# Plain sums in DRAM for three operand sets, merge gates loaded ahead, and later pool differences in a fused attention and pooling layer

## The chip, the cores and the metric

The kernel runs on one core of one Trainium2 chip. The metric is device time in microseconds (us) of the whole program. Before the change it took 1887.97 us, the median of 3 runs (1885.35 to 1888.47).

## The reference, cut to what matters

One layer over x (2048 x 1024): a modulated input u, one wide projection of u, sliding-window attention and a multi-scale causal pooling beside each other, each gated and projected, merged by sigmoid gates, projected out and normalized.

```python
u = x * (1.0 + scale[:, None, :]) + shift[:, None, :]
h = u @ w_in[l]
q, k, v, a_gate, p_in, p_gate, m_a, m_p = jnp.split(h, offsets, axis=-1)
a = sliding_window_sink_attention(q, k, v, sinks[l], bias, mask) * jax.nn.silu(a_gate)
a = a @ w_attn_proj[l]
p = jnp.einsum('bsgc,gcd->bsgd', multiscale_causal_pool(p_in), w_pool_mix[l]).reshape(B, S, POOL_WIDTH)
p = (p * pool_scale[l]) * jax.nn.silu(p_gate)
p = p @ w_pool_proj[l]
y = jax.nn.sigmoid(m_a) * a + jax.nn.sigmoid(m_p) * p
y = (y @ w_out[l]) * (1.0 + gate[:, None, :])
x = layer_norm(DEEPNORM_ALPHA * x + y, ln_gain[l], ln_bias[l])
```

The pooling subtracts from a mean over the last 2, 4, 8 or 16 positions (by group of channels) the value itself.

## The kernel before

**Products.** Every large matrix product is done in f32 precision from two fp32r parts, hi and lo, with three matmuls for each pair of 128x128 weights and 128x512 operand (`mm3`). The operand side is laid out as *sets*: seven sums of quarters of a matrix (B11, T1, T2, B21, T3, B22, T4), so that four output pieces come from seven products in place of eight. A set is a tile of 128 x 4 x 2 x 512: four row blocks, hi and lo. One product of a set is 12 matmuls. There is one buffer for each set, so a set of the next stage is filled when the last product of this stage has read it. The weight side is a *quad* (`class Quad`): W and A22 are loaded, POOL makes the sums (`sum1`, `mid`, `late`), and `pair_split` or `half_split` makes hi on ScalarE (ACT) and lo on VectorE (DVE) into tiles named w_set.

**Stages.** head; a first ring (g0) of five groups of two quads over the first half of the sequence; attention (a0); a second ring (g1) for the second half, with the two last gate quads of the first half in front of it ("post"); attention (a1); then "mix": the post quads, attention projection and pool projection of the first half (ain0, pin0) and of the second (ain1, pin1), and the output projection (wo) with the normalization. u1, ain0, pin0, ain1, pin1, wo also name the DRAM stores of the operands of those stages; g1 works on u1.

**The order in a ring.** `back` runs the products of a group: T2 and B21 of both quads, then T3 and B22 of each, then T4, 10 in all; `front` runs B11 and T1 of the next group's two quads. After each product comes a tick, and tables hang work on ticks: `sums_to` (four row blocks for each store, some 13 ticks each) loads two tiles named spare, second_qs or second_kk, lets POOL make the T sums in place and puts the results into a store; `planned` fills the sets of the next stage by `PLAN`. A store is either *split* (u1, wo, ain0: hi and lo in DRAM, made by `kept_parts`, into k_hi and k_lo from the ring "c" of five buffers unless a "parts" room is free; fetched by `fill_set` with 1 MB a transfer) or *plain* (pin0, ain1, pin1: f32 sums, 512 KB a fetch, cast by ACT and subtracted by DVE in the set itself, at the ticks of `FETCH_AT` and `SPLIT_AT`). The gate tiles (sig, ga, gp) use the ring "c" as well. Engines called through `act`, `dve`, `pool`, `sp` keep the program's order; calls through `nc` may be moved by the scheduler. Nearly all transfers are issued by SyncE (SP), one after the other.

**Attention.** 64 units of two heads and 128 queries, with 3 more to drain, interleave scores, softmax, transposes and values with steps of filler quads: pool input ("mix"), gates, and q. A mix quad gives four pieces. `take_p` handles one: `first` copies it from PSUM with 16 columns of history into vb (ACT) and POOL adds shifted copies, one to four times by window, into a tile "fin"; `second`, a unit later, has DVE subtract the piece from the mean and POOL multiply by the gate; a unit later it is stored to pin. `pool_free` starts pieces at least a unit apart. `seed` copies into a fresh PSUM bank, for which the bank of the quad's second piece must be free (`free_b`). There are four PSUM banks "mm". `take_gate` copies a gate's piece into a tile "raw", from where it is stored.

**Merge.** In mix, `attn_quad` and `pool_quad` load, for each of four output pieces, a stored gate (ma or mp), apply a sigmoid where it was stored raw, and multiply the piece by it, all at the piece's own place.

Of the kernel before, what the change touches and what calls it, by code (L numbers as in the profile page):

```python
# [12 lines left out]
F32 = mybir.dt.float32  # L13
# [46 lines left out]
def kernel(  # L60
# [56 lines left out]
    def split_store(name):  # L117
        return {n: dp.tile([4, P, 2, CH], F32, name=f"{name}_{n}_split") for n in set_names}

    u1_d = split_store("u1")  # L120
    wo_d = split_store("wo")
    ain0_d = split_store("ain0")
# [76 lines left out]
    def fill_set(name, half, src, eng=None):  # L199

        dst = as32(sets[name][:, 2 * half : 2 * half + 2])
        (eng or nc.sync).dma_start(dst, src[2 * half : 2 * half + 2].rearrange("i p h c -> p i h c"))

# [3 lines left out]
    def kept_parts(ph, dst, src):  # L207

        t = []

        def split():
            at = ph.turn_of("parts")
            if at:
                t.extend(at)
            else:
                t.extend(ph.c(n, F32R) for n in ("k_hi", "k_lo"))
            act.copy(t[0], src())
            low(dve, t[1], src(), t[0])

        def keep():  # L220
            for h in range(2):
                sp.dma_start(dst[:, h, :], as32(t[h]))

        return split, keep

    def sums_to(ph, store, i, load, work=None):

        b, split_too = [], store["B11"].shape[0] == 4
# [22 lines left out]
        raw = () if not split_too else ((4, "B11", (0, 0)), (5.4, "B21", (1, 0)), (6.1, "B22", (1, 1)))  # L251
        for at, name, z in (
            *raw, (8.5, "T1", (0, 1)), (10, "T2", (1, 1)), (11.5, "T4", (1, 0)), (13, "T3", (0, 0)),
        ):
            if split_too:
                split, keep = kept_parts(ph, store[name][i], lambda z=z: x(*z))
                todo += [(at, split), (at + 1, keep)]
            else:
                todo.append((at + 0.6, lambda name=name, z=z: put(sp, store, name, i, x(*z))))
# [10 lines left out]
    class Quad:  # L270
# [4 lines left out]
        def __init__(self, srcs, consume):  # L275
            self.srcs, self.consume = srcs, consume
# [319 lines left out]

    def attn_quad(s, m):
        def consume(ph, mi, t, src):
            k = m + mi
            g = ph.c("ga")  # L600
            nc.sync.dma_start(g, gates_d["ma"][s, k, t])
            nc.scalar.activation(g, g, AF.Sigmoid)
            if k not in ta:
                ta[k] = wide(ph, k)
            nc.vector.tensor_tensor(ta[k][:, t * CH : (t + 1) * CH], src, g, ALU.mult)

        return Quad((wap[m], wap[m + 1]), consume)

    def pool_quad(s, m):
        def consume(ph, mi, t, src):  # L610
            g = ph.c("gp")
            nc.sync.dma_start(g, gates_d["mp"][s, m + mi, t])
            if m < 4:
                nc.scalar.activation(g, g, AF.Sigmoid)
# [7 lines left out]
        return Quad((wpp[m], wpp[m + 1]), consume)  # L622
# [127 lines left out]
    def attention(ph, s, fills, post, opened):  # L750
# [28 lines left out]
        def pool_sums(m, t, acc):  # L779
            g = m // 2  # L780
            w = POOL_W[g]
            vb = tp.tile([P, 16 + CH], F32, tag="vb", bufs=1, name="vb")
# [17 lines left out]
            return cur  # L800

        pool_free, free_b = [0], [0]
# [4 lines left out]
        def take_p(m, t, acc):  # L807
            n = pool_free[0] = max(now_n[0], pool_free[0] + 1)
            x = []

            def first():
                x.append(ld("pg", gates_d["pg"][s, m, t], 2))
                x.append(pool_sums(m, t, acc))
# [745 lines left out]
```

## Time and profile before

| | |
|---|---|
| median of 3 runs | 1887.97 us |
| profiled execution | 1886.14 us |
| its span, first to last instruction | 1884.3 us |
| mean granted TensorE clock | 0.958 |
| PE, DVE, ACT, POOL busy | 91%, 65%, 52%, 56% |
| moved by DMA | 378.75 MB, mean 201 GB/s |

PE is TensorE, PEld its weight loads; POOL is GpSimd; SPq is SyncE's queue of instructions that issue transfers. Line L56 is a helper that records operations, so groups are told by their tiles: `mm<-set_B,w_set` is a product with one of the B sets into a bank of the ring "mm", `lg<-set_T,w_set` one with a T set. A number in brackets behind a row of the timeline is the idle time of the engine before it, with what ended it.

### The profile page before, as it was taken

What the parts mean: (1) busy time and instruction counts of PE and PEld (TensorE: products, weight loads), DVE (VectorE), ACT (ScalarE), POOL (GpSimd) and SP (SyncE); (2) the same over time, 40 slices, a digit from 0 to 9 for tenths busy, and PEclk for the clock granted to TensorE, in tenths of its full rate; (3) what the DMA queues carried; (4) which work ended last, traced back from release to release, by engine and by line L of the source; (5) the groups of instructions that cost most, each with busy time, mean ns of one, the idle gap of its engine ahead of it and who ended that gap; (6) DMA issues with size and microseconds to landing.
All of it is one profiled execution on the core that took longest, in us unless ns stands there. A gap on an engine that the chain in (4) does not pass through costs nothing.

```text
span 1884.3 us, 24950 instructions
## 1 busy us (share of the span) xinstructions
PE 1713.3 (91%) x8056; PEld 1418.5 (75%) x8056; DVE 1231.1 (65%) x2270; ACT 974.2 (52%) x2044; POOL 1062.8 (56%) x810
## 2 busy tenths in 40 slices
PE   6899999999998975749999999998998989999997
PEld 6688778888787864537888887887876767878785
DVE  6977756767675554655657777676346566755777
ACT  4644556767575532334457776665425334622452
POOL 2253438677768443545457859587365665354542
PEclk9999999999998997879999999999999989999998
DMA  8589753233423598788343234323899586779532
GB/s 325 190 280 333 226 187 122 92 107 129 140 80 111 202 326 288 277 283 298 115 164 128 96 111 140 102 90 118 295 381 333 162 288 221 245 241 381 199 134 101
DMA packets 199666, 378.75 MB, mean 201 GB/s; under 512 B 19424, under 2 KB 45168, under 8 KB 199536
## 3 DMA queue, kind: packets, MB, share of 16 engines
q1 hardware_dynamic: 196416, 372.91, 57.4%
q10 hardware_dynamic: 3088, 4.23, 0.9%
q8 instruction: 64, 1.05, 0.2%
q14 instruction: 66, 0.54, 0.1%
q0 software_dynamic: 32, 0.02, 0.0%
HBM read 245.79 MB, written 134.44 MB: 202 GB/s over the span
## 4 chain that ended last, share of the span: by engine, by line
PE 32%; POOL 6%; DMA 6%; DVE 5%; issue 3%; ACT 1%; SPq 1%; POOLq 0%; DVEq 0%; ACTq 0%
PE mm L56 20%; PE lg L56 10%; DVE w_set L135 1%; PE pv L56 1%; PE pt L56 1%; POOL w_set L56 1%; POOL nxt L56 1%; POOL fin L56 1%; DMA ain_T<-spare 1%; DMA W<-in_wpp_dram 1%; POOL wide L617 1%; ACT w_set L325 1%; DMA spare<-ain_B 1%; DMA A<-in_wap_dram 0%; DMA W<-in_wap_dram 0%
## 5 line engine op out<-in xcount | busy, mean ns | idle before, releaser
L56 PE MATMUL mm<-set_B,w_set 128*128 128x512 f32 x2664 | 681.0, 403 | 55.4 <-ACT w_set L325 29.7
L56 PEld LDWEIGHTS mm<-set_B,w_set 128*128 128x128 f32 x2664 | 508.2, 194 | 176.1 <-ACT w_set L325 33.4
L56 PE MATMUL mm<-set_T,w_set 128*128 128x512 f32 x1824 | 464.0, 401 | 27.8 <-DVE mm L56 12.5
L56 PE MATMUL lg<-set_T,w_set 128*128 128x512 f32 x1728 | 433.4, 402 | 46.0 <-DMA set_T<-u_T_split 15.7
L56 PEld LDWEIGHTS lg<-set_T,w_set 128*128 128x128 f32 x1728 | 333.2, 194 | 125.6 <-ACT lg L368 16.2
L56 PEld LDWEIGHTS mm<-set_T,w_set 128*128 128x128 f32 x1824 | 341.0, 191 | 103.9 <-DVE mm L56 16.9
L135 DVE TENSOR_TENSOR w_set<-W,w_set 128x1024 fp32r<-128x1024 f32 x138 | 197.6, 1432 | 202.7 <-ACT w_set L325 184.1
L56 POOL TENSOR_TENSOR w_set<-W,w_set 128x512 fp32r<-128x512 f32 x160 | 208.8, 1312 | 158.2 <-ACT w_set L56 152.7
L325 ACT CAST w_set<-W 128x1024 fp32r<-128x1024 f32 x138 | 144.6, 1049 | 263.8 <-PE mm L56 151.8
L288 POOL TENSOR_TENSOR W<-W,A 128x512 f32<-128x512 f32 x46 | 68.8, 1495 | 314.2 <-ACT sig L585 64.3
L56 ACT ACTIVATE L<-L,nm 128x257 f32<-128x257 f32 (+1 forms) x256 | 127.1, 498 | 27.6 <-DVE nm L56 21.9
L56 POOL TENSOR_TENSOR spare<-spare 128x512 f32<-128x512 f32 x68 | 117.1, 1724 | 28.1 <-DVE spare L56 13.0
L297 POOL TENSOR_TENSOR W<-W 128x512 f32<-128x512 f32 x46 | 66.9, 1455 | 109.8 <-DVE w_set L135 100.6
L56 DVE CUSTOM_DVE_ANT_0 L<-lg,bt,nsink 128x256 f32<-128x256 f32 (+1 forms) x256 | 111.6, 473 | 20.2 <-PE lg L56 10.9
L56 DVE COPY o<-pv 64x256 f32<-64x256 f32 x128 | 54.3, 424 | 105.4 <-PE pv L56 104.0
L56 ACT CAST pth<-pt 128x512 fp32r<-128x512 f32 (+1 forms) x128 | 72.9, 569 | 81.5 <-PE pt L56 81.0
L56 ACT ACTIVATE L<-L,sm 128x256 f32<-128x256 f32 (+1 forms) x128 | 64.3, 503 | 94.6 <-DVE sm L56 94.3
L56 ACT CAST w_set<-W 128x512 fp32r<-128x512 f32 (+1 forms) x164 | 100.4, 626 | 23.6 <-POOL W L56 10.0
L56 POOL TENSOR_TENSOR W<-W 128x512 f32<-128x512 f32 x82 | 105.1, 1296 | 4.2
L292 POOL TENSOR_TENSOR W<-W 128x512 f32<-128x512 f32 x44 | 74.0, 1682 | 43.2 <-DVE w_set L135 33.5
L56 DVE TENSOR_TENSOR ptl<-pt,pth 128x512 fp32r<-128x512 f32 (+1 forms) x128 | 85.7, 669 | 5.6 <-ACT pth L56 5.5
L293 POOL TENSOR_TENSOR W<-W 128x512 f32<-128x512 f32 x44 | 71.8, 1631 | 23.4 <-DMA W<-in_win_dram 18.6
(232 smaller groups left out, 2464.0 us busy)
## 6 DMA issues: line engine op xcount, KB each, us to landing
W<-in_win_dram SPq DMA_DIRECT2D x42, 512.0 KB, 5.6
W<-in_win_dram SPq DMA_DIRECT2D x42, 256.0 KB, 3.8
A<-in_win_dram SPq DMA_DIRECT2D x42, 256.0 KB, 4.1
ag_d<-sig SPq DMA_DIRECT2D x32, 256.0 KB, 4.7
pg_d<-sig SPq DMA_DIRECT2D x32, 256.0 KB, 4.4
pg<-pg_d SPq DMA_DIRECT2D x32, 256.0 KB, 3.1
pin_B<-fin SPq DMA_DIRECT2D x32, 256.0 KB, 2.1
ag<-ag_d SPq DMA_DIRECT2D x32, 256.0 KB, 3.0
```

The costliest lines, as they stand in the source:

```text
L56: return lambda *args, **kw: self.tc.keep_in_program_order(op(*args, **kw))
L135: engine.tensor_tensor(dst, src, as32(hi), ALU.subtract)
L288: e.tensor_tensor(self.w[:, 1, :], self.w[:, 2, :], self.a22, ALU.add)
L292: e.tensor_tensor(x[:, 1, :], x[:, 1, :], x[:, 0, :], ALU.subtract)
L293: e.tensor_tensor(x[:, 2, :], x[:, 0, :], x[:, 2, :], ALU.subtract)
L297: e.tensor_tensor(x[:, 3, :], x[:, 3, :], x[:, 1, :], ALU.subtract)
L325: a.copy(by_two(hi), raw)
L617: nc.gpsimd.tensor_tensor(dst, g, dst, ALU.add)
```

## The change

1. u1, wo and ain0 are kept as plain sums. `kept_parts`, `fill_set` and the "parts" rooms are gone; their sets are fetched and split by the path that pin0, ain1 and pin1 had. `sums_to` stores B11, B21 and B22 too where it worked on them (u1, wo), and stores at slightly other ticks.
2. `back` first calls `ahead` of each quad: the group's eight merge gates are loaded together, and their sigmoids made, into a ring of 8 buffers (5 before).
3. `take_p`: for windows of 8 and 16 the subtraction comes two units after `first`. A piece also starts at least three units after the one before the last. The quad's second piece is subtracted from its copy in vb (now two buffers), and `free_b` is a unit earlier. "raw" has no buffer of its own; it shares the two of "fin".

```diff
-    u1_d = split_store("u1")
-    wo_d = split_store("wo")
-    ain0_d = split_store("ain0")
+    u1_d = set_store("u1")
+    wo_d = set_store("wo")
...
-        raw = () if not split_too else ((4, "B11", (0, 0)), (5.4, "B21", (1, 0)), (6.1, "B22", (1, 1)))
+        made = ((4, "B11", (0, 0)), (5, "B21", (1, 0)), (6, "B22", (1, 1))) if work else ()
         for at, name, z in (
-            *raw, (8.5, "T1", (0, 1)), (10, "T2", (1, 1)), (11.5, "T4", (1, 0)), (13, "T3", (0, 0)),
+            *made, (8.6, "T1", (0, 1)), (10.1, "T2", (1, 1)), (11.6, "T4", (1, 0)), (13.1, "T3", (0, 0)),
         ):
-            if split_too:
-                split, keep = kept_parts(ph, store[name][i], lambda z=z: x(*z))
-                todo += [(at, split), (at + 1, keep)]
-            else:
-                todo.append((at + 0.6, lambda name=name, z=z: put(sp, store, name, i, x(*z))))
+            todo.append((at, lambda name=name, z=z: put(sp, store, name, i, x(*z))))
...
     def back(ph, grp, opened, nxt, own, tick):
         st = []
+        for turn in range(2):
+            for q in grp:
+                if q.ahead:
+                    q.ahead(ph, turn)
...
-        if store["B11"].shape[0] == 4:
-            return [(p, lambda n=n, h=h: fill_set(n, h, store[n])) for p, n, h in PLAN]
...
+    def gates_ahead(name, s, m, raw):
+        g = {}
+
+        def ahead(ph, turn):
+            for mi, t in (((0, 0), (1, 1)), ((0, 1), (1, 0)))[turn]:
+                x = g[mi, t] = ph.c("g")
+                sp.dma_start(x, gates_d[name][s, m + mi, t])
+                if raw:
+                    nc.scalar.activation(x, x, AF.Sigmoid)
+
+        return g, ahead
...
-            vb = tp.tile([P, 16 + CH], F32, tag="vb", bufs=1, name="vb")
+            vb = tp.tile([P, 16 + CH], F32, tag="vb", bufs=2, name="vb")
...
-            n = pool_free[0] = max(now_n[0], pool_free[0] + 1)
+            n = max(now_n[0], pool_free[1] + 1, pool_free[0] + 3)
+            pool_free[:] = pool_free[1], n
+            wait = 1 if POOL_W[m // 2] < 8 else 2
+            own = (m % 2, t) == (0, 1)
...
-                dve.scalar_tensor_tensor(p, p, 1.0 / POOL_W[m // 2], acc, ALU.mult, ALU.subtract)
+                dve.scalar_tensor_tensor(
+                    p, p, 1.0 / POOL_W[m // 2], copied if own else acc, ALU.mult, ALU.subtract
+                )
                 pool.tensor_tensor(p, p, pg, ALU.mult)
-                later(n + 2, lambda: keep_raw(pin_d[s], m, t, p))
-
-            later(n + 1, second)
-            if (m % 2, t) == (0, 1):
-                free_b[0] = n + 1
+                later(n + wait + 1, lambda: keep_raw(pin_d[s], m, t, p))
+
+            later(n + wait, second)
+            if own:
+                free_b[0] = n
...
-                x = tp.tile([P, CH], F32, tag="raw", bufs=1, name="raw")
+                x = tp.tile([P, CH], F32, tag="fin", bufs=2, name="raw")
...
-        ph.turns["parts"] = cycle([[cols(x, n) for n in range(2)] for x in kq[2:]] + [None])
+        ph.turns["spare"] = cycle([None, None, *(as32(x) for x in kq[2:])])
...
-    with Pools("mix", spare=4, p=2, c=5) as ph:
+    with Pools("mix", spare=4, p=2, c=8) as ph:
```

Where instructions stand now. First ACT in g1, at the end of the first group and the opening of the next (sig: a gate's piece; w_set: a hi part of weights, from W or from A; k_hi: a hi part that is stored; second_qs, second_kk: tiles that `sums_to` works on). Before:

```order
L585 ACTIVATE sig<-mm 128x512
L56 CAST k_hi<-second_qs_6624 128x512
L56 CAST k_hi<-second_qs_6626 128x512
L325 CAST w_set<-W 128x1024
L585 ACTIVATE sig<-p_6952 128x512
L56 CAST k_hi<-second_qs_6624 128x512
L585 ACTIVATE sig<-mm 128x512
L56 CAST k_hi<-second_qs_6627 128x512
L56 CAST k_hi<-second_kk 128x512
L369 COPY p_7391<-mm 128x512
L325 CAST w_set<-W 128x1024
```

After:

```order
L56 CAST set_T_573<-set_T_573 128x2x512
L555 ACTIVATE sig<-mm 128x512
L293 CAST w_set<-W 128x1024
L56 CAST set_T_573<-set_T_573 128x2x512
L293 CAST w_set<-W 128x1024
L555 ACTIVATE sig<-mm 128x512
L555 ACTIVATE sig<-p_6821 128x512
L300 CAST w_set<-A_6615 128x512
L555 ACTIVATE sig<-mm 128x512
L300 CAST w_set<-A_6662 128x512
```

The k_hi casts between the weight splits are gone, and the last of the 14 casts of the set splits stand there; the groups behind this one have neither.

Next DVE in the first attention stage, at the end of the mix quad with window 16 (mm<-mm,p is the addition behind the product T2, fin the pool difference, sm, o and L,nm the softmax and output steps of a unit). Before:

```order
L56 TENSOR_TENSOR mm<-mm,p_5971 128x512
L56 SCALAR_TENSOR_TENSOR fin<-fin,p_5623 128x512
L56 RECIPROCAL sm<-sm 128x2
L56 COPY o_6087<-pv 64x256
L56 TENSOR_TENSOR o<-pv,o_6087 64x128 x2
L56 ISA L,nm<-lg,bt,nsink 128x256
```

After:

```order
L56 TENSOR_TENSOR mm<-mm,p_5847 128x512
L56 SCALAR_TENSOR_TENSOR fin<-fin,mm 128x512
L56 RECIPROCAL sm<-sm 128x2
L56 COPY o_5962<-pv 64x256
L56 TENSOR_TENSOR o<-pv,o_5962 64x128 x2
L56 ISA L,nm<-lg,bt,nsink 128x256
```

At this place the fourth piece's difference (from p) stood; now the third's (from mm) stands there, and the fourth's follows two units later.

Last SP in the mix stage, at the first groups of ain0 (ga and g: merge gates; ain_T<-spare: stores of T sums of the second half; W and A: weights of the next group). Before:

```order
L281 DMA W<-in_wap_dram 128x512
L282 DMA A_13343<-in_wap_dram 128x512
L283 DMA W<-in_wap_dram 128x2x512
L601 DMA ga<-ma_d 128x512 x2
L56 DMA ain_T_119<-spare 128x512
L281 DMA W<-in_wap_dram 128x512
L282 DMA A_13389<-in_wap_dram 128x512
L283 DMA W<-in_wap_dram 128x2x512
L601 DMA ga<-ma_d 128x512
L56 DMA ain_T_123<-spare 128x512
L601 DMA ga<-ma_d 128x512 x2
```

After:

```order
L56 DMA ain_T_111<-spare 128x512
L56 DMA ain_T_115<-spare 128x512
L56 DMA g<-ma_d 128x512 x8
L56 DMA ain_T_113<-spare 128x512
L56 DMA spare<-ain_B_112 128x512
L56 DMA spare<-ain_B_114 128x512
L249 DMA W<-in_wap_dram 128x512
```

The gate loads, spread over the group in ones and twos, now stand as one block of eight ahead of the weight loads of the next group.

More of the change, by code (lines that the diff above doesn't have):

```diff
@@ L197, in split_set @@
         low(d, lo, src, hi)
-    def fill_set(name, half, src, eng=None):
-        dst = as32(sets[name][:, 2 * half : 2 * half + 2])
-        (eng or nc.sync).dma_start(dst, src[2 * half : 2 * half + 2].rearrange("i p h c -> p i h c"))
     def put(q, store, name, i, src):
         q.dma_start(store[name][i // 2, :, i % 2, :], src)
[L207 to L214, printed above, removed]
-            else:
[L216 to L224, printed above, removed]
     def sums_to(ph, store, i, load, work=None):
-        b, split_too = [], store["B11"].shape[0] == 4
+        b = []
         def x(r, c):
@@ L1390, in second_phase @@
             ))
-        for raw, split in ((ain_d[0], ain0_d), (pin_d[0], pin_d[0])):
+        for raw in (ain_d[0], pin_d[0]):
             for i in range(4):
-                side.append(sums_to(ph, split, i, load_raw(raw, i)))
+                side.append(sums_to(ph, raw, i, load_raw(raw, i)))
         ahead, hooks = hooks, {}
```

33 lines of the change are left out of this document (13 added, 20 removed).

## The prediction

> **What bounds the kernel now.** I read the page, then one windows table over the stages, then the waits and the timeline where TensorE (PE) stands. A row of the table gives: stretch in us, its length, busy us (instructions) of PE, PEld, DVE, ACT and POOL, granted PE clock, DMA share, GB/s.
>
> ```profile
> span 1884.3 us, 24950 instructions
> ```
> ```profile
> 80.00:280.00 200.00, 191.50 (x930) 159.39 (x928) 146.71 (x168) 104.33 (x163) 84.92 (x51) 1.00 0.81 269
> 280.00:640.00 360.00, 345.59 (x1825) 295.82 (x1826) 245.93 (x700) 235.72 (x655) 272.13 (x226) 0.98 0.34 110
> 640.00:680.00 40.00, 39.98 (x178) 32.83 (x177) 17.84 (x22) 16.91 (x24) 14.52 (x10) 1.00 0.96 338
> 680.00:880.00 200.00, 133.00 (x473) 100.92 (x472) 115.30 (x118) 71.43 (x111) 89.10 (x57) 0.82 0.85 291
> 880.00:960.00 80.00, 79.07 (x343) 64.49 (x344) 45.41 (x52) 35.76 (x55) 37.30 (x29) 0.98 0.52 174
> 960.00:1320.00 360.00, 345.98 (x1847) 295.60 (x1846) 247.76 (x696) 240.70 (x656) 267.21 (x215) 0.99 0.34 112
> 1320.00:1440.00 120.00, 115.82 (x506) 93.89 (x504) 53.67 (x62) 44.86 (x63) 57.67 (x40) 0.99 0.90 331
> 1440.00:1600.00 160.00, 137.17 (x551) 108.73 (x550) 104.01 (x93) 69.51 (x92) 106.79 (x63) 0.91 0.72 246
> ```
>
> PE is the bound nearly everywhere: it is idle 8.5 us of 200 in the first ring stage (g0, 80 to 280), 14.4 and 14.0 us in the two attention stages (280 to 640, 960 to 1320). It is not the bound from 680 to 880, in the second ring stage (g1): 133.0 busy of 200, at a granted clock of 0.82. No other engine is full there either; the DMA engines are at 0.85.
>
> What g1 should take follows from its products of 12 matmuls, here its first two and its last in the timeline of PE (start, us, what):
>
> ```profile
> 644.55 2.88 PE L56 MATMUL lg<-set_T,w_set 128*128 128x512 f32 x12
> 647.27 2.88 PE L56 MATMUL mm<-set_B,w_set 128*128 128x512 f32 x12
> ...
> 962.57 2.88 PE L56 MATMUL mm<-set_T,w_set 128*128 128x512 f32 x12
> ```
>
> Undisturbed, products start 2.72 us apart. By the code g1 has 10 + 4 of the two carried-over quads and the first group's front, 5 x 10 of the groups, and 4 x 4 + 2 of the following fronts: 82, or 223 us. From 644.55 to the end of the last, 965.29, it took 320.7: **97 us lost**. 67 of them are the idle time in 680 to 880, the rest mainly the slow clock behind the gaps. Who is waited for there (engine and line <- releaser, us, times, longest), for PE and for the queue that issues transfers (SPq):
>
> ```profile
> PE mm L56 <- ACT w_set L325: 24.0, 4, 8.5
> PE lg L56 <- DMA set_T<-u_T_split: 15.7, 4, 7.0
> ```
> ```profile
> SPq L56 <- DVE k_lo L56: 55.3, 35, 6.0
> SPq L56 <- ACT k_hi L56: 27.5, 21, 4.8
> ```
>
> The queue stood 82.8 us for hi and lo parts that the kernel stores, with the weight loads behind them in it. One such place, in the timeline (in brackets the idle time before, and what ended it):
>
> ```profile
> 739.99 1.27 POOL L288 TENSOR_TENSOR W<-W,A 128x512 f32<-128x512 f32 x1 [24.75 <-DMA A<-in_win_dram]
> ...
> 749.48 0.62 ACT L56 CAST k_hi<-second_kk 128x512 fp32r<-128x512 f32 x1 [4.46 <-DMA wo_T_split<-k_lo]
> ...
> 758.29 4.19 PE L56 MATMUL mm<-set_B,w_set 128*128 128x512 f32 x8 [7.79 <-ACT w_set L325]
> ```
>
> POOL had to wait for a weight load; ACT, in order, held a k_hi cast until an earlier store had released a ring buffer, with the weight split that PE needs behind it.
>
> **The change part by part.** A. *Plain sums instead of parts.* A tile of 128x512 f32 is 256 KB; a set (8 tiles split, 4 plain) is 2.1 MB split and 1.05 MB plain. In g1, reading seven u1 sets saves 7.3 MB, storing seven wo sets 7.3 MB, and ain0 shrinks from 14.7 MB to 4.2 (the T sets alone; its B sets stand in DRAM already). That is 25.2 MB of the 85.6 that rows 640 to 960 moved (338 x 40 + 291 x 200 + 174 x 80 us). The 60.4 MB left are 246 GB/s over 246 us, below the 269 at which g0 lost 8.5 us in 200. Also gone from g1 are 56 k_hi casts, 56 k_lo subtractions and 68 of 112 store issues; new are 14 set splits, which cost what today's plain sets do (ns: min/median/max):
>
> ```profile
> L56 DVE TENSOR_TENSOR k_lo<-second_qs,k_hi x28: 677/692/1778, 693.9 to 860.5; 128x512 fp32r<-128x512 f32 x28
> ```
> ```profile
> L56 ACT CAST set_T<-set_T x24: 1027/1046/1052, 1423.7 to 1649.2; 128x1024 fp32r<-128x1024 f32 x24
> L56 DVE TENSOR_TENSOR set_T<-set_T x24: 1207/1218/2321, 1426.4 to 1655.8; 128x1024 fp32r<-128x1024 f32 x24
> ```
>
> At medians DVE sheds 56 x 0.69 = 39 us and takes on 14 x 1.22 = 17; since neither DVE nor ACT is near full, only the order matters. What stays of the 97 us: 10, at g0's rate of loss over 246 us; 11 in the opening, whose first 18 products (49 us) ask for u1 7.3 MB, wout 4, wo stores about 4, weights and gates about 5 (counted in the code), 20 MB, and at 338 GB/s that is 60 us; 6 for set splits that stand before other work. 27 stay, **70 gained**. Ends: 38, if each of the opening's seven sets comes as late as the longest wait for one above (49 in place of 11 and 6, rounded), and 87, if the opening is hidden.
>
> Fetches of both sizes have rows (KB each, median us to landing):
>
> ```profile
> set_T<-u_T_split SPq DMA_DIRECT2D x8, 1024.0 KB, 8.7
> ...
> set_T<-pin_T SPq DMA_DIRECT2D x16, 512.0 KB, 5.7
> ```
>
> Half the bytes land in 66% of the time, not 50. Counted by landing, reading u1 saves 34% of 14.7 MB, 5.0 MB in place of 7.3; 2.3 MB at 291 GB/s are 8 us, and A is 62. I keep 70, since SP issues ahead and what a full queue delays is bytes; 62 lies in the range.
> The Trainium skill, DMA: Bandwidth & Descriptors (Bandwidth), advises batches of at least 1 MiB for 75% of peak, which speaks against halving these fetches. The trace agrees in direction.
>
> In g0, 28 tiles fewer are split and half the bytes stored: 2 us of its 8.5, ends 0 and 6.
>
> B. *Pool differences.* In attention DVE waits in order for the running sums on POOL, four adds long where the window is 16 (waits of the whole span, then the timeline):
>
> ```profile
> DVE fin L56 <- POOL fin L56: 55.2, 18, 6.5
> ```
> ```profile
> 582.56 0.69 DVE L56 SCALAR_TENSOR_TENSOR fin<-fin,mm 128x512 f32<-128x512 f32 x1 [4.91 <-POOL fin L56]
> ...
> 587.02 1.65 PE L56 MATMUL mm<-set_T,w_set 128*128 128x512 f32 x3 [4.80 <-DVE mm L56]
> ```
>
> Behind it on DVE are the softmax steps and the addition that PE waits for. A unit later (360 us / 67 units, 5.4 us) the sum is done, as 4.91 is less than a unit. A quad's first piece then keeps its PSUM bank until unit 33 (mix 4, taken in 31), and PE begins the product that reuses it in 34: covered by a unit; without that cover PE would wait what DVE waits now. The second piece's bank is free after ACT's copies. Next late are the sums' buffers: "raw" now shares the two of "fin", so ACT's raw copies (units 6, 7, 36, 39, 56, 59 of each stage) and POOL's fourth sum wait for a store issued in the same or the next unit. No row shows this; it is between 0 and the 4.80 of PE above, at 12 places. I take 0.5 each, since PE's weight splits run three products ahead: 28.4 us of idle time become 7 left over and 6 of these, **15 gained**; ends -30 (12 x 4.80 against the 28.4) and 24.
>
> C. *Gates a group ahead; splits at ain0 and wo* (waits of ACT, then the timeline):
>
> ```profile
> ACT gp L614 <- DMA gp<-mp_d: 30.8, 8, 7.7
> ACT ga L602 <- DMA ga<-ma_d: 22.6, 10, 6.2
> ```
> ```profile
> 1456.55 1.21 DVE L56 TENSOR_TENSOR set_B<-set_B 128x1024 fp32r<-128x1024 f32 x1
> ...
> 1460.69 4.63 PE L56 MATMUL mm<-set_T,w_set 128*128 128x512 f32 x12 [5.38 <-DVE wide L605]
> ```
>
> From 1320 to 1600 PE is idle 27.0 us. ACT's 53 us of waiting for gates go, most of them off PE's path: I take 10 of the 27. The lighter queue in 1320 to 1440 (0.90 busy, 331 GB/s) gives 3 of the 4.2 there. Against it, ain0 and wo bring 14 splits each to stage changes that had none. At 1460 PE waited for a gate product that stood on DVE behind set splits such as the one at 1456; half of that 5.38 at two changes is -5. **8 gained**; ends -10 (both whole, no gain from gates) and 22.
>
> **The sum.** 70 + 2 + 15 + 8 = 95. The profiled execution took 1886.1 us (the span and 1.8 around it): 1791. The median of the runs shown, 1888.0, lies 1.9 above it: **1793**.
>
> **Rivals.** *Everything goes* (0.12): A 87, g0 6, B 20, C 15, so 1760. For it: 60.4 MB at 338 GB/s need 179 of 246 us. Against: the opening asks for more than that rate.
>
> *Set splits hold ACT and DVE* (0.15). They stand in program order, fetched only three or four products ahead, and beside them each side slows: set_T subtractions took 1218 ns at the median and up to 2321. If 28 of the 42 new ones each lose that 1.1 us on PE's path, it is 31, so 1824. For it: the row 1440 to 1600, 22.8 us idle around two such stage changes. Against: in 1320 to 1440 DVE is busy 54 of 120.
> The Trainium skill, SBUF — State Buffer (Who interferes with whom), has a DVE operation with two SBUF inputs and a POOL operation that reads SBUF exclude each other. The trace agrees, with its 2321 against 1218.
>
> *The shared buffers cost what the later difference saves* (0.10): 12 places at 3.8 us are 45 where I count 6; B is -24 and the time 1832. Against: the store is issued within a unit of its sum.
>
> *Slower* (0.04): eight gate loads stand as a block in SP's order at the head of eight groups, ahead of weight loads, and the last needs the buffer that the group before releases with its last consumer. If that blocks, weights come late as at 739.99 and PE waits 7.79 as at 758.29. At 16 quads it decides from 95 / 16 = 5.9 us each; at 7.79 it is 125, so 1918. Against: that consumer is some four products (11 us) before the block.
>
> **How the numbers follow.** The forecast, with its own range of 1765 to 1815, holds 0.59; the rivals have the chances above. I give 1793 and the range 1762 to 1838: it takes in the forecast, the second and third rival and the upper part of the first. 0.2% (4 us) is about what a measurement of this kernel can tell from no change. Faster 0.95, same 0.01, slower 0.04.
>
> **What would show it.** Right: in g1 no gap of PE over 4 us after its first 60; SP's waits for k_lo and k_hi gone; DVE's wait for fin under 15 us; ACT's for gates under 15. Wrong: in g1's opening ACT waiting over 20 us for set fetches, and PE for w_set behind it; ACT raw or POOL fin waiting for a pin_B store; POOL W waiting for weights behind "g" loads. Above 1856 (B and C at their lower ends) A itself has failed.

## The result and the profile after

The changed kernel takes 1762.21 us, the median of 4 runs (1761.71 to 1762.30), against 1886.66 us before (4 runs): a ratio of 0.9345, interval 0.9324 to 0.9365. The profiled execution took 1762.15 us. So 124 us went where the forecast had 95. The time stands 31 us below the number given, 0.2 us above the lower end of the range, and 3 us below the 1765 to 1815 that the forecast took as its own.

To see where it went, both traces are laid beside each other product by product: the products are the same and stand in the same order, so a stage is the time from the start of its first product to the start of the next stage's first. "Attention" is both attention stages.

| us | head | g0 | attention | g1 | mix | span |
|---|---|---|---|---|---|---|
| before | 80.6 | 198.6 | 731.4 | 322.1 | 551.6 | 1884.3 |
| after | 81.3 | 191.4 | 716.2 | 242.9 | 528.5 | 1760.3 |
| gained | -0.7 | 7.1 | 15.2 | 79.2 | 23.1 | 124.0 |
| predicted | 0 | 2 | 15 | 70 | 8 | 95 |

First the stretches of after, in the windows table (columns as in the prediction: stretch, length, busy us and instructions of PE, PEld, DVE, ACT, POOL, granted clock, DMA share, GB/s). Its third to fifth row are g1:

```profile
80.00:271.00 191.00, 189.02 (x926) 159.02 (x925) 120.17 (x137) 88.16 (x131) 79.43 (x50) 1.00 0.73 239
271.00:632.00 361.00, 350.34 (x1856) 298.72 (x1855) 248.80 (x707) 239.95 (x661) 278.02 (x228) 0.98 0.35 114
632.00:672.00 40.00, 40.00 (x177) 32.98 (x177) 28.08 (x26) 26.91 (x35) 15.28 (x10) 1.00 0.94 337
672.00:792.00 120.00, 108.60 (x454) 87.99 (x453) 75.41 (x69) 39.78 (x57) 98.73 (x62) 0.96 0.83 294
792.00:873.00 81.00, 81.00 (x363) 67.06 (x362) 42.67 (x53) 37.20 (x57) 31.69 (x23) 1.00 0.46 151
```

g1 moves 61.0 MB (337 x 40 + 294 x 120 + 151 x 81 us) where the prediction counted 60.4. In g1 PE stands only in the middle row, for 11.4 us, and the clock there is 0.96 where it was 0.82. The first and last product of g1, and the two long gaps, in the timelines of PE and of DVE (in brackets the idle time before, and what ended it):

```profile
631.83 2.88 PE L56 MATMUL lg<-set_T,w_set 128*128 128x512 f32 x12
...
677.59 4.38 PE L56 MATMUL mm<-set_B,w_set 128*128 128x512 f32 x11 [4.49 <-DVE set_B L56]
...
695.09 4.29 PE L56 MATMUL mm<-set_B,w_set 128*128 128x512 f32 x11 [4.71 <-DVE set_B L56]
...
870.61 2.88 PE L56 MATMUL mm<-set_T,w_set 128*128 128x512 f32 x12
```
```profile
670.80 4.53 DVE L56 TENSOR_TENSOR second_qs<-second_qs,cb 128x1024 f32<-128x1024 f32 x2
675.26 2.28 DVE L56 TENSOR_TENSOR set_B<-set_B 128x1024 fp32r<-128x1024 f32 x1
```

From 631.83 to 873.33 (the last start and 2.72) it is 241.5 us for 82 products, 18.5 over the ideal 223, where 97 were lost before. At both gaps PE waits for a set split that stands on DVE behind the scaling of wo. It does not wait for a fetch: ACT waits for those of u1 1.3 us (T sets) and 0.8 us (B sets) in all.

Then the waits of the whole span that the prediction named (engine, line <- releaser: us, times, longest):

```profile
DVE fin L56 <- POOL fin L56: 6.2, 6, 2.0
ACT g L575 <- DMA g<-ma_d: 9.6, 5, 5.3
ACT g L575 <- DMA g<-mp_d: 3.1, 1, 3.1
ACT set_T L56 <- DMA set_T<-u_T: 1.3, 2, 0.9
ACT raw L56 <- DMA pin_B<-fin: 31.9, 5, 9.3
```

DVE's 55.2 us for the running sums are 6.2, ACT's 53 us for gates are 12.7, and the fetches of u1's T sets make ACT wait for 1.3; SP's waits for k_lo and k_hi are gone with these tiles. Of the signs of being right one is missed by little: the second long gap of PE in g1 ends 63.3 us into it. The last row is new, and the prediction had named it as a sign of being wrong: ACT waits for a store of pool differences before it may write raw. One such place in attention, in the timelines of ACT and PE:

```profile
470.59 0.59 ACT L56 COPY raw<-mm 128x512 f32<-128x512 f32 x1 [7.77 <-DMA pin_B<-fin]
...
472.87 0.56 ACT L56 CAST pth<-pt 128x512 fp32r<-128x512 f32 x1
```
```profile
473.49 0.58 PE L56 MATMUL pv<-pth,vv 128*128 128x256 f32 x1 [3.61 <-ACT pth L56]
```

Behind the raw copy on ACT stand a weight split, the copies of the next pool piece and the softmax's pth, and PE waits 3.61 us for that.

### The profile page after: what moved, and what is told of

The parts are those of the page before. It is cut to its first block, busy times and chain, and to the rows that moved or that the text cites. A ratio compares the mean times of both kernels' runs of the same rounds, so it can differ in the third digit from the quotient of the medians.

```text
span 1760.3 us, 24568 instructions
## 1 busy us (share of the span) xinstructions
PE 1673.0 (95%) x8056; PEld 1396.0 (79%) x8056; DVE 1219.1 (69%) x2228; ACT 964.7 (55%) x2002; POOL 1087.6 (62%) x810
## 4 chain that ended last, share of the span: by engine, by line
PE 42%; POOL 8%; DVE 7%; DMA 5%; issue 4%; ACT 3%; SPq 0%; POOLq 0%; DVEq 0%; ACTq 0%
PE mm L56 27%; PE lg L56 12%; PE pv L56 2%; DVE w_set L131 2%; PE pt L56 1%; POOL spare L56 1%; POOL w_set L56 1%; POOL wide L597 1%; DMA set_T<-ain_T 1%; DVE set_T L56 1%; POOL W L256 1%; DMA W<-in_wpp_dram 1%; POOL fin L56 1%; DMA g<-mp_d 1%; DVE set_B L56 1%
## 5 line engine op out<-in xcount | busy, mean ns | idle before, releaser
L56 PE MATMUL mm<-set_B,w_set 128*128 128x512 f32 x2664 | 665.0, 397 | 21.9 <-DVE set_B L56 9.2
L56 PEld LDWEIGHTS mm<-set_B,w_set 128*128 128x128 f32 x2664 | 501.8, 191 | 134.1 <-DVE w_set L131 11.4
L56 PE MATMUL mm<-set_T,w_set 128*128 128x512 f32 x1824 | 457.8, 397 | 7.2 <-POOL w_set L56 4.1
L56 PE MATMUL lg<-set_T,w_set 128*128 128x512 f32 x1728 | 422.6, 395 | 18.3 <-DVE w_set L131 9.2
L56 PEld LDWEIGHTS mm<-set_T,w_set 128*128 128x128 f32 x1824 | 337.3, 189 | 79.4 <-POOL w_set L56 6.3
L56 PEld LDWEIGHTS lg<-set_T,w_set 128*128 128x128 f32 x1728 | 325.6, 190 | 93.5 <-DVE w_set L131 14.5
L56 ACT ACTIVATE L<-L,nm 128x257 f32<-128x257 f32 (+1 forms) x256 | 127.1, 498 | 21.9 <-DVE nm L56 15.6
L265 POOL TENSOR_TENSOR W<-W 128x512 f32<-128x512 f32 x46 | 73.1, 1589 | 99.4 <-DVE w_set L131 88.2
L56 POOL TENSOR_TENSOR spare<-spare 128x512 f32<-128x512 f32 x64 | 112.6, 1762 | 5.1 <-DVE spare L56 2.2
L56 POOL TENSOR_TENSOR W<-W 128x512 f32<-128x512 f32 x82 | 109.8, 1352 | 4.2
L260 POOL TENSOR_TENSOR W<-W 128x512 f32<-128x512 f32 x44 | 73.4, 1672 | 40.7 <-DVE w_set L131 31.6
L261 POOL TENSOR_TENSOR W<-W 128x512 f32<-128x512 f32 x44 | 75.6, 1718 | 22.2 <-DMA W<-in_win_dram 14.3
L56 DVE TENSOR_SCALAR L<-L,sm 128x256 f32<-128x256 f32 (+1 forms) x128 | 88.9, 695 | 0.0
```

What stands on the lines that cost most here:

```text
L56: return lambda *args, **kw: self.tc.keep_in_program_order(op(*args, **kw))
L260: e.tensor_tensor(x[:, 1, :], x[:, 1, :], x[:, 0, :], ALU.subtract)
L261: e.tensor_tensor(x[:, 2, :], x[:, 0, :], x[:, 2, :], ALU.subtract)
L265: e.tensor_tensor(x[:, 3, :], x[:, 3, :], x[:, 1, :], ALU.subtract)
```

## The experiments

All times of a run's stages are in one table, worked out as above; the medians are of 4 runs or 5.

| us | median | g0 | attention | g1 | mix |
|---|---|---|---|---|---|
| sums_alone | 1780.98 | 190.2 | 730.7 | 244.2 | 535.5 |
| pool_alone | 1871.59 | 197.6 | 715.8 | 322.6 | 551.3 |
| gates_alone | 1873.62 | 199.2 | 730.7 | 322.3 | 540.8 |
| no_gates | 1770.26 | 191.7 | 716.4 | 245.3 | 534.4 |
| bytes_back | 1795.31 | 190.8 | 715.3 | 275.2 | 529.2 |
| casts_back | 1787.56 | 190.1 | 715.9 | 268.7 | 528.9 |
| both_back | 1821.02 | 193.4 | 716.6 | 298.2 | 528.9 |
| hi_only | 1816.62 | 197.5 | 732.4 | 268.0 | 534.1 |
| raw_nxt2 | 1749.70 | 190.8 | 702.7 | 242.9 | 528.7 |
| wait_1 | 1763.15 | 190.4 | 715.2 | 243.5 | 527.7 |
| early_first | 1760.76 | 191.0 | 716.6 | 244.5 | 525.6 |
| best | 1761.69 | 192.5 | 701.6 | 243.3 | 541.0 |

**The three parts alone.** sums_alone is the kernel before with part 1 of the change (stores, sums_to, set_steps, the spare rooms, ain0's phase):

```diff
...
-    u1_d = split_store("u1")
-    wo_d = split_store("wo")
-    ain0_d = split_store("ain0")
+    u1_d = set_store("u1")
+    wo_d = set_store("wo")
...
```

> The kernel before with the plain sums alone (u1, wo, ain0 as f32 sums, split where used); the pool differences and the gates as they were. The traces of before and after, laid beside each other product by product, give the gain of the whole change as 7.1 us in g0, 79.0 in g1, 15.2 in the two attention stages and 23.0 in mix. If the parts add up (main theory), this one has g0 and g1 whole, nothing in attention, and in mix at most what its smaller ain0 and wo fetches bring: 1795 to 1805 us, g1 near 242 us. My prediction's size for it, 72 gained, would be 1815. Rival: the plain sums need the later pool differences or the gates ahead to pay, since 42 new set splits stand among the waits that those remove; then g1 stays over 260 us or mix gets slower, and the time is 1815 to 1840.

Measured: 1780.98 us, ratio 0.9433 (0.9398 to 0.9468): 104.5 us below before, more than either theory. g0 and g1 have their whole gain without the other parts, so the rival falls. And mix gains 16.1 of its 23.1, although it has 28 of the new set splits and the gates are as they were.

pool_alone has part 3 alone (take_p, vb, free_b, raw in the buffers of fin):

```diff
...
-            n = pool_free[0] = max(now_n[0], pool_free[0] + 1)
+            n = max(now_n[0], pool_free[1] + 1, pool_free[0] + 3)
...
-                x = tp.tile([P, CH], F32, tag="raw", bufs=1, name="raw")
+                x = tp.tile([P, CH], F32, tag="fin", bufs=2, name="raw")
```

> The kernel before with the later pool differences alone. Main theory: 15 us of the gain, as the two attention stages show in the traces (365.4 to 359.1 and 366.0 to 357.2), so 1871 to 1873 us, g1 unchanged near 320. Rival: part of those 15 us comes from what the plain sums left behind at the border of the stages (fewer transfers still running when attention begins), then 1876 to 1883.

Measured: 1871.59 us, ratio 0.9919 (0.9889 to 0.9950), 13.9 us; attention gains 15.6, g1 and mix stay. The part stands by itself. Its waits already show both sides of it, as in after:

```profile
DVE fin L56 <- POOL fin L56: 6.2, 6, 2.0
ACT raw L56 <- DMA pin_B<-fin: 32.1, 4, 9.2
```

gates_alone has part 2 alone, and no_gates, run later, is the kernel after without it:

```diff
...
+        for turn in range(2):
+            for q in grp:
+                if q.ahead:
+                    q.ahead(ph, turn)
...
-    with Pools("mix", spare=4, p=2, c=5) as ph:
+    with Pools("mix", spare=4, p=2, c=8) as ph:
```

> The kernel before with the merge gates loaded a group ahead alone (ring of 8 buffers in mix). Theory one: the 23 us that mix gained (551.6 to 528.5) are the gates', as PE no longer waits behind gate loads on ACT and DVE: 1862 to 1866 us. Theory two (the prediction's sizes): gates bring about 13 and the rest of mix's gain belongs to the smaller ain0 and wo sets: 1872 to 1876. Rival: the block of eight loads on SP takes back what it saves where the set fetches stand behind it: 1880 or more.

> The kernel after with the merge gates loaded at their own places as before, in a ring of 5. Laid apart, mix takes 551.6 us before, 535.5 with the plain sums alone, 540.8 with the gates alone and 528.5 with both. Theory one, the gates are worth 7 us beside the plain sums: 1767 to 1771 us, mix near 535.5. Theory two, what the gates gained alone (11 to 12) holds here too and the difference in the runs apart is scatter: 1773 to 1776. Rival: the block of eight costs in pin0 what the gates gain elsewhere: within 3 us of 1762.

Measured: gates_alone 1873.62 us, ratio 0.9919 (0.9890 to 0.9948), 11.9 us, by theory two; no_gates 1770.26 us, ratio 0.9373 (0.9351 to 0.9395), 8.1 above after, by theory one. By these times the gates are worth 8 to 12 us; by mix alone they are 5.9 beside the other parts (534.4 to 528.5) and 10.8 alone. The intervals of no_gates and after overlap a little, their runs do not (1767.42 to 1771.24, 1761.71 to 1762.30). 16 of mix's 23 belong to the plain sums. The three parts apart add to 104.5 + 13.9 + 11.9 = 130.3 us, 6 more than together, which is within the spread of the runs before (1881.07 to 1888.47).

**What g1 lost its time to.** bytes_back puts the transfers back and no work:

```diff
...
+            if store is wo_d or store is ain_d[0]:
+                todo.append((at, lambda z=z: sp.dma_start(next(again_d), x(*z))))
+        if store is ain_d[0]:
+            for at, z in ((4, (0, 0)), (5, (1, 0)), (6, (1, 1))):
+                todo += [(at, lambda z=z, n=n: sp.dma_start(next(again_d), x(*z))) for n in range(2)]
...
             sp.dma_start(raw(name, half), store[name][half])
+            if store is u1_d:
+                sp.dma_start(as32(sets[name][:, 2 * half : 2 * half + 2, 0, :]), store[name][half])
```

> The kernel after, with the 25.2 MB that the change took out of g1 put back as transfers alone: each store to wo and ain0 is made twice, six more stores for each row block of ain0 stand where the B parts were stored, and each u1 fetch is made twice (the second into the hi half of the set, which the cast then overwrites). No cast or subtraction comes back. Theory bytes: g1 lost its time to bytes on the DMA engines and to the queue behind them, so g1 goes from 241.5 us back to 290 to 325 and the time to 1810 to 1845. Theory order: g1 lost it to k_hi and k_lo work that waited for ring buffers ahead of the weight splits; then the bytes alone cost little, g1 stays under 260 and the time under 1780.

Measured: 1795.31 us, ratio 0.9512 (0.9482 to 0.9542); g1 275.2. That is 32.3 us of the 79.2, between the two theories. Its windows, for the opening and the middle of g1:

```profile
632.00:672.00 40.00, 34.15 (x141) 27.33 (x140) 20.59 (x22) 20.48 (x27) 10.53 (x8) 0.91 1.03 382
672.00:792.00 120.00, 90.69 (x351) 70.80 (x350) 55.92 (x55) 35.23 (x49) 65.22 (x44) 0.87 1.03 378
```

With the bytes back and nothing that holds SP, the DMA engines are full at 378 to 382 GB/s. The kernel before did not reach that in g1 (0.96 and 338 GB/s in its first 40 us, 0.85 and 291 in the stretch where PE lost most), so more than bytes was at work in it.

casts_back puts the work back and no transfers:

```diff
...
+            def parts(z):
+                t = [ph.c(n, F32R) for n in ("k_hi", "k_lo")]
+                act.copy(t[0], x(*z))
+                low(dve, t[1], x(*z), t[0])
...
```

> The kernel after, with the 56 hi casts on ACT and the 56 lo subtractions on DVE of the stores to wo and ain0 put back at the ticks of before, into the same ring of five buffers that the gates use; nothing is stored from them. So the work of before is there, without its bytes and without a transfer that waits for it or that it waits for. Theory A, separate costs: the work is the other 47 us of the 79, so g1 takes 280 to 290 us and the time is 1800 to 1812. Theory B, coupled: the work alone costs little, since its buffers come free as soon as DVE is done; g1 under 255 us and the time under 1778.

Measured: 1787.56 us, ratio 0.9483 (0.9464 to 0.9501); g1 268.7, so the work alone is 25.8 us, again between the theories. One of its windows, PE's two longest waits in g1, and half of its k_lo subtractions (ns: min/median/max):

```profile
672.00:792.00 120.00, 91.41 (x347) 69.72 (x346) 114.01 (x104) 61.65 (x97) 86.04 (x47) 0.87 0.69 233
```
```profile
PE lg L56 <- DVE w_set L131: 14.9, 6, 7.2
PE mm L56 <- DVE set_B L56: 10.7, 3, 6.5
```
```profile
L56 DVE TENSOR_TENSOR k_lo<-second_qs,k_hi x28: 675/966/1776, 678.7 to 787.4; 128x512 fp32r<-128x512 f32 x28
```

DVE is busy 114.0 of 120 us, and PE's longest waits are for it: at the faster pace it is the bound. These k_lo, 692 ns at the median before, take 966 here. By the trace this goes with POOL: of all 56, the 13 with no POOL instruction beside them take 0.68 us at the median, the 43 with one 1.16.

both_back has both edits at once, still without what is called the tie below: SP's queue waiting for a cast, and a cast waiting for a ring buffer that a store still holds.

```diff
...
+                todo.append((at, lambda z=z: sp.dma_start(next(again_d), x(*z))))
...
+                todo.append((at, lambda z=z: parts(z)))
...
```

> The kernel after, with both the bytes and the casts put back in g1 as in the two runs before, but still apart: no transfer waits for a cast, and no ring buffer for a transfer. Measured so far, g1 takes 322 us before, 243 after, 275 with the bytes back, 279 with the casts back, and 268 in the kernel before with the lo parts neither stored nor fetched. Theory one, the two costs add and the tie between cast, ring buffer and store is a third cost: g1 near 311 (243 + 32 + 36), time 1828 to 1834, and the 11 us left to before are the tie. Theory two, the two costs need no tie to make up the whole: g1 at 318 or more, time 1836 to 1845. Theory three, they hide behind each other: g1 under 300, time under 1820, and the tie is worth over 20 us.

(The expectation gives g1 with the casts back as 279; the table has 268.7, so theory one is 243 + 32 + 26 = 301.) Measured: 1821.02 us, ratio 0.9645 (0.9617 to 0.9673); g1 298.2. The two costs add (55.3 against 58.1). What is left to the 322.1 of before, 24 us, I put down to the tie, by subtraction: no run adds the tie alone. It is rather more than 24 if the set splits of g1, which both_back has and before had not, cost anything there.

hi_only goes at it from the other side, and leaves the lo parts out of the products:

```diff
...
-            for h in range(2):
-                sp.dma_start(dst[:, h, :], as32(t[h]))
+            sp.dma_start(dst[:, 0, :], as32(t[0]))
...
-        dst = as32(sets[name][:, 2 * half : 2 * half + 2])
-        (eng or nc.sync).dma_start(dst, src[2 * half : 2 * half + 2].rearrange("i p h c -> p i h c"))
+        dst = as32(sets[name][:, 2 * half : 2 * half + 2, 0, :])
+        (eng or nc.sync).dma_start(dst, src[2 * half : 2 * half + 2, :, 0, :].rearrange("i p c -> p i c"))
```

> The kernel before with all its k_hi and k_lo work, but only the hi part is stored and fetched for u1, wo and ain0 (the lo part of these operands is left out, so the products lack it). Bytes and transfers fall as in the change, the casts, their ring buffers and their places stay. With the bytes put back the kernel after lost 32 us in g1, of the 79 that g1 gained. Theory A, two separate costs: bytes are 32 of the 79, so g1 takes 285 to 295 us here, and with some 5 to 8 in g0 and up to 16 in mix the time is 1830 to 1845. Theory B, one coupled cost: casts and transfers hold each other up (ACT waits for a ring buffer until a store has landed, SP waits for the cast), and taking either away frees both; then g1 is under 265 us and the time under 1815. Theory C, the casts alone: g1 stays over 300.

Measured: 1816.62 us, ratio 0.9629 (0.9591 to 0.9666); g1 268.0, just outside theory B. SP still stands for casts, here in its waits in g1:

```profile
SPq L56 <- ACT k_hi L56: 72.2, 39, 7.1
```

And yet g1 is as long as in casts_back, where nothing is tied (268.7, with 14 set splits that hi_only does not have). So with half the bytes, what is left of the tie costs no more than those splits. It is less of a tie, too: no store waits for DVE's k_lo any more, for which SP stood 55.3 us before. Whether the bytes behind the queue or those stores make the 24 us was not told apart. g0 gains 1.1 here of the 8.4 of sums_alone: in g0 it was not the bytes, but the work or SP's waits for it. In mix it is the other way: 534.1 with half the bytes and no new set splits, 535.5 with them. There the bytes are 17.5 us, and the 28 set splits cost 1.4, no more than the traces that leave mix as it is in after differ (527.7 to 529.2).

**Attention.** raw_nxt2 takes the gates' raw tile out of fin's two buffers:

```diff
-                x = tp.tile([P, CH], F32, tag="fin", bufs=2, name="raw")
+                x = tp.tile([P, 16 + CH], F32, tag="nxt2", bufs=1, name="raw")[:, 16:]
```

> The kernel after, with the gates' raw tile in the buffer nxt2 (a step of the running sums of windows 8 and 16 only) in place of the two buffers of fin. In the trace of after ACT waits 31.9 us at 5 places for a pin_B store that holds fin, with weight splits and the softmax copies behind it, and PE stands behind four of them: 3.8 us at 469, 1.4 at 585, 1.8 at 1073 and 3.1 at 1182, 10 us in all. Theory one: that is the price of sharing, and it goes: 1752 to 1755 us, ACT's wait for pin_B under 3 us. Theory two: sharing is hidden and something else ends there next: within 3 us of 1762. Rival: nxt2 makes POOL wait for the raw store in its turn, and the pool differences come late: 1764 or more.

Measured: 1749.70 us, ratio 0.9282 (0.9264 to 0.9300), apart from the 0.9345 of after; attention 702.7, 13.5 us less, where the expectation had 10 at the most. ACT's wait for pin_B is gone; what is left before raw, in its waits:

```profile
ACT raw L56 <- POOL nxt L56: 6.8, 3, 2.8
ACT raw L56 <- POOL fin L56: 4.4, 2, 2.8
```

wait_1 undoes the later difference in that kernel:

```diff
-            wait = 1 if POOL_W[m // 2] < 8 else 2
+            wait = 1
```

> The kernel raw_nxt2 (1749.7 us) with the pool differences of windows 8 and 16 back at one unit after the first step, all else of the change to them kept (the copy in vb, the earlier bank, the spacing). In the traces DVE waits 55.2 us for the sums before the change and 6.2 after it. Theory one, the later difference is what gains in attention: DVE's wait for fin rises over 35 us and the two attention stages by 12 to 26 together, 1762 to 1776 us. Theory two, the spacing of the pieces (at least three units after the one before the last) and the copy are what gains: within 4 us of 1750.

Measured: 1763.15 us, ratio 0.9338 (0.9314 to 0.9362); attention 715.2, 12.5 us more. In its waits DVE stands for the sums longer, 32.6 us against 15.4 in raw_nxt2, though they stay under the 35 that the expectation had:

```profile
DVE fin L56 <- POOL fin L56: 32.6, 17, 3.8
```

So attention, from 731.4 to 702.7 without the shared buffers, gains 28.7: 12.5 by the later difference, 16.2 by the spacing, the copy, the earlier bank and raw's other buffer together, which were not told apart.

**The block of gate loads.** In after, SP, ACT and PE at the change from pin0 to ain1, in their timelines:

```profile
1395.71 5.66 SPq L56 DMA_DIRECT2D g<-mp_d  x8
1402.01 1.19 SPq L56 DMA_DIRECT2D set_B<-ain_B  x2
```
```profile
1408.54 1.05 ACT L56 CAST set_B<-set_B 128x1024 fp32r<-128x1024 f32 x1 [11.88 <-DMA set_B<-ain_B]
...
1413.87 1.04 ACT L293 CAST w_set<-W 128x1024 fp32r<-128x1024 f32 x1
```
```profile
1414.97 1.09 PE L56 MATMUL lg<-set_T,w_set 128*128 128x512 f32 x2 [4.16 <-ACT w_set L293]
```

The block goes out ahead of the fetches, ACT stands for them, and the weight split that PE needs stands behind. early_first spreads the gates and puts the sets' work first on each tick:

```diff
...
             if gi + 1 < len(groups):
+                gates(ph, groups[gi + 1], 0)
                 opened = [front(ph, q, tick) for q in groups[gi + 1]]
...
             tick()
+            if not n:
+                gates(ph, grp, 1)
...
-            for f in hooks.get((pos[0], pos[1]), ()):
-                f()
             for f in hooks.get((pos[0] - len(groups), pos[1]), ()):
                 f()
+            for f in hooks.get((pos[0], pos[1]), ()):
+                f()
...
```

> The kernel after, with two changes of order: the first four gates of a group are loaded before the products that open it, the other four after its first product (in place of all eight in one block at its head), and on each tick the fetches and splits of the next stage's sets come ahead of the side work. In the trace of after SP issues the block for 5.7 us from 1395.7 on, the ain1 set fetches go out behind it at 1402, ACT waits 11.9 us for them with a weight split behind it, and the second group of pin0 takes 53.5 us where the kernel with the plain sums alone took 47.0; in g1's opening PE waits twice (4.5 and 4.7 us) for a set split that stands on DVE behind the scaling of wo. Theory one: the block and the order are the cause: pin0's second group falls to 46 to 49 us, g1 by 6 to 9, and the time to 1746 to 1752. Theory two: the set fetches are late because SP stands for a sum of POOL, and the splits because DVE is full there: within 4 us of 1762.

Measured: 1760.76 us, ratio 0.9340 (0.9321 to 0.9359), not to be told from after. pin0's second group does fall, from 53.5 to 46.9 us, and pin1 by 2.2; ain0 rises by 4.7 and ain1 by 3.3, and g1 does not fall.

best keeps raw_nxt2 and cuts the block in two:

```diff
...
-        for turn in range(2):
-            for q in grp:
-                if q.ahead:
-                    q.ahead(ph, turn)
+        gates(ph, grp, 0)
...
             tick()
+            if not n:
+                gates(ph, grp, 1)
...
```

> The kernel raw_nxt2 (1749.7 us) with the block of eight gate loads cut in two: four at the head of the group, four after its first product, so that the set fetches of the next stage stand behind four in place of eight. In early_first the second group of pin0 fell from 53.5 to 46.9 us, but the first group of ain0 rose by 4.7 and ain1 by 3.3, where the gates had gone ahead of the opening products; this one leaves those in place. Theory one, the block is what holds the ain1 fetches: pin0's second group falls to 47 to 50 us and nothing rises, 1743 to 1748 us. Theory two, SP stands for POOL's sums there and the block only fills the time: within 2 us of 1750.

Measured: 1761.69 us, ratio 0.9330 (0.9309 to 0.9351), 12 above raw_nxt2; pin0's second group 54.1, ain0 up by 6.0 and ain1 by 8.6. At the same place its timelines read:

```profile
1391.48 2.94 SPq L56 DMA_DIRECT2D g<-mp_d  x4
1394.80 1.19 SPq L56 DMA_DIRECT2D set_B<-ain_B  x2
```
```profile
1400.82 1.05 ACT L56 CAST set_B<-set_B 128x1024 fp32r<-128x1024 f32 x1 [10.12 <-DMA set_B<-ain_B]
```
```profile
1404.22 1.22 PE L56 MATMUL lg<-set_T,w_set 128*128 128x512 f32 x2 [7.41 <-ACT w_set L293]
```

The fetch now stands behind four loads, and ACT still waits 10.1 us for it, PE longer than before. Neither theory holds: the block's length is not all that makes that fetch late, and where the gates go in this queue changes single stage changes by 2 to 9 us, up or down. Two parts of the wait do not hang on the block: a fetch takes 6.8 us to land in after and 6.4 in best, and ahead of the block SP had stood for a sum of POOL (8.6 us in after, 3.8 in best). What sets the fetch there stays open. The fastest kernel of the study is raw_nxt2.

## Why the prediction was right, and where it was not

**The sum.** A came out 9 us above its size, g0 5, C 15, and the head 1 below: these are the 29 between 95 and 124. B's size came by two errors. The range reached down to 1762 only because it took in part of the first rival; that the time lies in it owes as much to luck as to the working.

**A, the plain sums in g1: right, its size short.** The 97 us lost were worked out rightly, and 61.0 MB against 60.4 too (the 246 us that these were spread over have no working; 223 and the 27 left are 250). 18.5 stay where 27 were left. The term that failed is the 11 us of the opening: at 0.94 and 337 GB/s PE was busy 40.00 of 40 us. In the opening's 49 us 17.1 MB went (348 GB/s) where I had counted 20, and no product waited for a fetch; what became of the other 3 MB of the count is not known. The 10 us at g0's rate did not come either. What did come is the third term, set splits behind other work: put at 6 us, it is 9.2 by the two rows of PE. Another 2 us are smaller gaps, and the rest, 7, goes by products that run slower, as those behind the gaps do (4.38 and 4.29 us for 11 matmuls, where 12 take 2.88). The upper end of 87 dropped the 6 together with the 11; with the opening alone hidden it is 81, and 79 came. The check by landing times pointed the wrong way: a u1 fetch of half the size landed in 7.0 us against 8.7, 80% where I had 66% from other rows, and the stage gained more, not less.

```profile
set_T<-u_T SPq DMA_DIRECT2D x8, 512.0 KB, 7.0
```

The Trainium skill, DMA: Bandwidth & Descriptors (Bandwidth), has its advice of 1 MiB a batch right in direction: by these two rows one fetch, from issue to landing, moves fewer bytes in a us at half the size. The stage gained all the same, 32 us by fewer bytes and 26 by less work, and that rule doesn't speak of these.

**A, its mechanism: one sentence was wrong.** "Since neither DVE nor ACT is near full, only the order matters." The busy shares that carried it came from a stretch in which PE stood a third of the time. At the pace after the change the same 56 subtractions, beside the new set splits, fill DVE to 114.0 of 120 us, and with their casts cost 25.8 us with no transfer tied to them. The loss was 32 of bytes, 26 of work and, by subtraction, 24 or more of the tie between them. The Trainium skill, SBUF — State Buffer (Who interferes with whom), has a DVE operation with two SBUF inputs and a POOL operation that reads SBUF exclude each other; the k_lo of casts_back, 1.16 us beside POOL and 0.68 without, agree, and so does set_B at 2.28 us.

**g0: 2 us predicted, 7 measured.** My 2 us stood for 28 tiles fewer to split and half the bytes stored. By hi_only the bytes give 1.1; the rest comes with the 28 tiles that ACT and DVE no longer split and that SP no longer waits for, which no run takes apart.

**B: 15 predicted, 15.2 measured, by two errors that cancel: the number is luck.** The place of the gain and the place of the price were both named rightly. (A unit of 5.4 us did not cover every wait for a sum, as the row before has one of 6.5; 6.2 us of these waits are left.) But the gain without the shared buffers is 28.7, where I took 21.4 (28.4 less 7); and only 12.5 of it come by the later difference, which I had as the whole, and 16.2 by the rest of part 3. The sharing costs 13.5, where I took 12 places at 0.5 us. It is not a small price at all places but a large one at few: ACT waited at 5, up to 9.3 us. "PE's weight splits run three products ahead" was the wrong cover: behind the raw copy on ACT stands pth, which PE needs in the same unit. The third rival, 45 us for sharing, had the mechanism and three times the size.

**C: 8 predicted, 23 measured in mix.** The gates themselves were put nearly right: 10 predicted, 6 to 8 measured beside the rest, 11 to 12 alone. The step that failed is what part A brings to mix: 3 for a lighter queue and -5 for set splits, so -2, against +16.1 in sums_alone. By hi_only the lighter fetches of ain0 and wo are worth 17.5 and the splits cost hardly anything (1.4). I read the lighter queue only against the 4.2 us that PE was idle from 1320 to 1440, where the DMA engines were at 0.90; but what that queue delays shows later. In sums_alone 5.2 of the 16 us come in the second group of ain0 and 9.9 in the opening and first group of pin0, a stage further on.

**The rivals.** "Everything goes" gave 1760 and the time is 1762, but with other terms: A 79 for 87, B 15 for 20, and 23 in mix for 15; its argument, that the bytes fit, holds for the opening, where PE lost nothing in the first 40 us. "Set splits hold ACT and DVE" is there at two places in g1, 9.2 us in place of 31. The slower one did not come: the block of gate loads delays one stage change by 5 us, as no_gates shows (pin0's second group 48.7 against 53.5), and gives more back in the others.

## What to carry to other kernels

A resource's busy share in a stage that is slowed by something else says little about the share once that is gone: work it out at the pace that you predict. Bytes, work and the tie between them are separate prices; put one of them back at a time, alone, to see which it was, and look for what a lighter queue is worth in the stages behind the one where it is full. When two tiles of different users share a ring of buffers, price the longest hold of the one at each use of the other, and ask what stands behind the wait in that engine's order.

## What the runs showed of the hardware that was not expected

PE lost nothing over 40 us in which the DMA engines were at 0.94 and 337 GB/s; at 1.03 and 382 GB/s, in bytes_back, it stood 5.9 of 40. A queue whose head waits 72 us for casts in hi_only cost g1 little against one that doesn't wait; in the kernel before, with the bytes of both parts and stores that waited 55.3 us for DVE as well, 24 us or more are left for it by subtraction. A 128x1024 set subtraction on DVE took 1.22 us at the median with no POOL instruction beside it and 2.31 with one (24 each of set_T in after).
